# Buffers from the general pool for the first weight splits at three stage borders, and no split ordered behind the residual, in a two-layer encoder on one core

## The chip, the core and the metric

The kernel runs on one core of a Trainium2 chip. The metric is the device time of one execution in microseconds (us). The kernel before was run three times: 2235.65, 2235.11 and 2233.4 us, median 2235.11. PE is TensorE (the matmul engine), DVE VectorE, ACT ScalarE, POOL GpSimd, SP the engine whose queue issues the weight loads.

## The reference

Two layers of an encoder on 256 tokens of width 2048, in float32. Cut to what matters here:

```
for l in range(DEPTH):                       # DEPTH = 2
    h = rmsnorm(x, pre_mix_norm[l])
    proj = h @ w_in[l]                       # 2048 -> 4176, to three groups of heads
    mix = concatenate([o_a, o_b, o_c]) @ w_out[l]
    x = x + rmsnorm(mix, post_mix_norm[l])
    h = rmsnorm(x, pre_ffn_norm[l])
    f = (silu(h @ w_gate[l]) * (h @ w_up[l])) @ w_down[l]
    x = x + rmsnorm(f, post_ffn_norm[l])
```

All of x must be summed (rmsnorm over 2048 columns) before any row of the next stage's result is final. The kernel applies the row's scale behind the matmul, so that only the residual itself, not its sum of squares, stands ahead of the next stage's first matmul.

## The kernel before

**Precision.** Each float32 operand of a large matmul is split into a high and a low part in a format that PE takes at full rate: ACT casts it (`hi`), DVE subtracts (`lo = src - hi`). This is `hilo`, lines 327 to 329. A product then takes three matmuls: high x high, low x high, high x low.

**A dense product** (`dense`, from line 337) goes through its weights in units of 1024 columns (two chunks of 128 rows by 512 columns). `unit(u)` loads a unit into a `ws` buffer by SP, splits it into `wh` and `wl`, and `mm` (lines 347 to 355) issues the three matmuls of one chunk and one half of the tokens (t = 0 or 1, 128 tokens each). There are five buffers each of `ws`, `wh` and `wl` (`WSB`, `WHB`), and a general pool of 64 buffers of 512 columns (`U()`), from which activations and their splits come.

**At a stage's border** the old stage's last product is called with `tail=4`: its last four units keep their splits, all matmuls of half 0 come first, `residual(0)` runs on DVE while PE does half 1. The new stage's first product is called with `head=3`: its units 0 to 2 do half 0 alone, half 1 follows behind unit 2, so that PE has work while `residual(1)` runs. There are three such inner borders: mixing to channel mixer of layer 0 (near 399 us), layer 0 to layer 1 (near 1117 us), and mixing to channel mixer of layer 1 (near 1506 us). A unit of the new stage has six matmuls per half.

**The new x** becomes matmul input by quads: `norm_quad` (from line 435) transposes four blocks of 128 columns on PE (L439), multiplies by the gain, and splits. For the very first quad of half 0 it does this block by block (ACT L332, DVE L333), for all others by one DVE product (L448) and `hilo` (L328, L329). x has four quads in each half, eight in all.

**Order.** Each engine takes its instructions in the order that the build has written down. The build places them by its own view of what is ready and by the program's order; a tile's buffer is given in the order in which the program asks for one of that kind. Where the program says so, an instruction stands behind another one of its engine:

```
for u0, ins in hold:
    if u >= u0:
        order.enter_context(tc.issue_after(ins.ins))
hilo(wh[:, 0:m * n], wl[:, 0:m * n], ws[:, 0:m * n])
```

`hold` is set by `residual(0)` to its last operation, with u0 = 1: at an inner border the low halves of units 1 and 2 stand behind it on DVE. At the program's start `hold` has other entries (lines 112 and 523), which concern the very first product.

**The old stage's end on DVE.** In `out_proj` the evacuation adds the accumulator to the earlier part (L1201, where there are two passes), ACT squares it (L1204), DVE multiplies by the gain (L1205). `residual` then runs a chain of small operations for the row's scale (`rsqrt_sum`, L257 to L270) and four operations on 512 columns (L495).

Of the kernel before, what the change touches and what calls it, by code (L numbers as in the profile page):

```python
# [10 lines left out]
F32R = mybir.dt.float32r  # L11
I32 = mybir.dt.int32
AF = mybir.ActivationFunctionType
ALU = mybir.AluOpType
AX = mybir.AxisListType

P = 128
# [25 lines left out]
WHB = 5  # L43
# [10 lines left out]
def kernel(  # L54
# [8 lines left out]
    act, dve, pe, pool, sync = nc.scalar, nc.vector, nc.tensor, nc.gpsimd, nc.sync  # L63
# [3 lines left out]
    wpool = ctx.enter_context(tc.tile_pool(name="wpool", bufs=3))  # L67
# [5 lines left out]
    def U(dt=F32):  # L73
        return upool.tile([P, 512], dt, tag="u", name="u")
# [37 lines left out]
    hold = [(0, dve.tensor_copy(out=col0, in_=ps[:, 0:16]))]  # L112
# [139 lines left out]
    def rsqrt_sum(v, part, mul, eps, tag):  # L252

        pre = SM(1, tag + "p")
        dve.tensor_reduce(out=pre, in_=v, axis=AX.X, op=ALU.add)  # L257
        dve.tensor_scalar(out=pre, in0=pre, scalar1=eps / mul, scalar2=None, op0=ALU.add)
        w = SM(3, tag + "w")
        z = SM(1, tag + "z")  # L260
        a = SM(1, tag + "a")
        dve.tensor_scalar(out=w[:, 0:1], in0=part, scalar1=pre[:, 0:1], scalar2=64.0 * mul,
                          op0=ALU.add, op1=ALU.mult)
        dve.tensor_scalar(out=z.bitcast(I32), in0=w[:, 0:1].bitcast(I32), scalar1=-0.5,
                          scalar2=float(0x5F3759DF - 2 ** 31), op0=ALU.mult, op1=ALU.add)
        for i in range(1, 3):
            dve.tensor_scalar(out=w[:, i:i + 1], in0=w[:, 0:1], scalar1=4.0 ** -i, scalar2=None, op0=ALU.mult)
        for i in range(3):
            dve.scalar_tensor_tensor(out=a, in0=z, scalar=w[:, i:i + 1], in1=z, op0=ALU.mult, op1=ALU.mult)
            dve.scalar_tensor_tensor(out=z, in0=a, scalar=-3.0, in1=z, op0=ALU.add, op1=ALU.mult)  # L270
        return z
# [55 lines left out]
    def hilo(hi, lo, src):  # L327
        act.copy(out=hi, in_=src)  # L328
        dve.tensor_tensor(out=lo, in0=src, in1=hi.bitcast(F32), op=ALU.subtract)  # L329
# [7 lines left out]
    def dense(lhs, ks, n, load, evac, ch=2, need=None, pre=None, head=0, mid=None, tail=0,  # L337
              after0=None):

        acc = [psa.tile([P, 512], F32, tag="acc", name="acc") for _ in range(NT)]
        nu = -(-len(ks) // ch)
        held = []

        def mm(t, c, u, kc, wh, wl):
            i = u * ch + c
            rh = wh[:, c * n:(c + 1) * n]
            rl = wl[:, c * n:(c + 1) * n]  # L350
            xh, xl = lhs(kc[c], t)
            o = acc[t][:, 0:n]
            pe.matmul(o, xh, rh, start=(i == 0), stop=False)  # L353
            pe.matmul(o, xl, rh, start=False, stop=False)  # L354
            pe.matmul(o, xh, rl, start=False, stop=(i == len(ks) - 1))  # L355

        def unit(u):
            kc = ks[u * ch:(u + 1) * ch]
            m = len(kc)
            ws = wpool.tile([P, 1024], F32, tag="ws", name="ws", bufs=WSB)  # L360
            wv = ws[:, 0:m * n].rearrange("p (c n) -> p c n", c=m)
            load(wv, kc[0], m)
            wh = wpool.tile([P, 1024], F32R, tag="wh", name="wh", bufs=WHB)
            wl = wpool.tile([P, 1024], F32R, tag="wl", name="wl", bufs=WHB)
            with ExitStack() as order:
                if u < head:
                    for u0, ins in hold:
                        if u >= u0:
                            order.enter_context(tc.issue_after(ins.ins))
                hilo(wh[:, 0:m * n], wl[:, 0:m * n], ws[:, 0:m * n])  # L370
            if need is not None:
                for k in kc:
                    bg.ensure(*need(k))
            return u, kc, wh, wl

        for u in range(nu):
            a = unit(u)
            if head <= u < nu - tail:
                for c in range(len(a[1])):
                    for t in range(NT):  # L380
                        mm(t, c, *a)
            else:
                for c in range(len(a[1])):
                    mm(0, c, *a)
                held.append(a)
                if u == head - 1 and mid is not None:
                    mid()
                if u == nu - 1:
                    if pre is not None:
                        pre()  # L390
                        pre = None
                    evac(0, acc[0][:, 0:n])
                if u in (head - 1, nu - 1):
                    for h in held:
                        for c in range(len(h[1])):
                            mm(1, c, *h)
                    held.clear()
            bg.step(BUDGET)
        if pre is not None:
            pre()  # L400
        if after0 is not None:
            after0()
        for t in range(1 if tail else 0, NT):
            evac(t, acc[t][:, 0:n])
# [85 lines left out]
    def residual(t, parts, ssqp, rname):  # L490

        r = rsqrt_sum(ssqp[t][:, 0:3], ssqp[t][:, 3:4], 1.0 / DM, EPS, rname)
        for c in range(4):
            xv = xs[:, t, c * 512:(c + 1) * 512]
            ins = dve.scalar_tensor_tensor(out=xv, in0=parts[(c, t)], scalar=r[:, 0:1], in1=xv,  # L495
                                           op0=ALU.mult, op1=ALU.add)
        if t == 0:
            hold[:] = [(1, ins)]

    def post_weight(ap, l):  # L500
        w = [U() for _ in range(4)]
# [6 lines left out]
    for l in range(DEPTH):  # L508
# [677 lines left out]
        def out_proj(lhs, passes, w, wpm, rname, need, after0):  # L1186
            parts = {}
            ssqp = [SM(4, "ssqp0"), SM(4, "ssqp1")]
            for i, ks in enumerate(passes):
                last = i == len(passes) - 1  # L1190
                for nb in range(4):
                    if i == 0:
                        parts[(nb, 0)], parts[(nb, 1)] = U(), U()

                    def ev(t, ps):
                        o = parts[(nb, t)]
                        if not last:
                            act.copy(out=o, in_=ps)
                            return
                        if i > 0:  # L1200
                            dve.tensor_tensor(out=o, in0=o, in1=ps, op=ALU.add)  # L1201
                            ps = o
                        junk = U()
                        act.activation(out=junk, in_=ps, func=AF.Square, accum_out=ssqp[t][:, nb:nb + 1])  # L1204
                        dve.tensor_tensor(out=o, in0=ps, in1=wpm[nb], op=ALU.mult)  # L1205
                        if nb == 3:
                            residual(t, parts, ssqp, rname)
                    dense(lhs, ks, 512, wload(w, nb * 512, 512), ev, need=need,
                          **(dict(tail=TAILG, after0=after0) if last and nb == 3 else {}))
# [251 lines left out]
```

## Time and profile before

| | |
|---|---|
| runs | 2233.4 to 2235.65 us, median 2235.11 |
| profiled execution | 2234.73 us, its span 2233.0 us |
| mean granted clock of TensorE | 0.998 |
| busy: PE, PEld, DVE, ACT | 99%, 82%, 79%, 53% |
| chain that ended last: PE, DVE, DMA | 92%, 5%, 1% |

The page gives the busy time of each engine and the chain of work that ended last. Views of the trace give more: what an engine waited for, the instructions of an engine in order of time (start, duration, line, operation, output and inputs), and busy times in a stretch. "Busy" on PE is modelled from starts: back to back, matmuls of 512 columns start every 0.227 us, though each is shown with 0.39 us.

### The profile page before, as it was taken

The numbers are of one execution on the slowest core, as the hardware profiler recorded it, in microseconds if no ns is written. First come the engines' busy times: TensorE is split into PE (matmuls) and PEld (weight loads), VectorE is DVE, ScalarE is ACT, GpSimd is POOL, SyncE is SP. The second block draws the span as 40 slices with busy tenths as digits, with TensorE's granted clock in tenths as the row PEclk, the third lists the DMA queues.
The fourth block names the chain that finished last, engine by engine and source line by source line (L and its number), as shares of the span: only waits on it lengthen the run. The fifth ranks groups of instructions, "written<-read, shape, count | busy, mean of one in ns | idle before, by whom it ended". The sixth has DMA issues, their size and how long they took to land.

```text
span 2233.0 us, 29215 instructions
## 1 busy us (share of the span) xinstructions
PE 2203.0 (99%) x10483; PEld 1839.3 (82%) x10483; DVE 1762.0 (79%) x2873; ACT 1182.5 (53%) x1642; POOL 45.9 (2%) x93
## 2 busy tenths in 40 slices
PE   8999999999999999999999999999999999999998
PEld 7988887788888888888879888877888888888886
DVE  6777998899999897544486779979999998975444
ACT  6665545555555555444356655455555555554432
POOL 2000000000000000000000000000000000000000
PEclk9999999999999999999999999999999999999999
DMA  7554525546656656555556545245565566665553
GB/s 254 171 178 146 188 89 162 162 164 207 217 181 217 225 189 223 171 195 192 179 172 186 183 142 171 97 153 161 188 207 208 191 215 214 202 214 178 191 196 124
DMA packets 218545, 407.75 MB, mean 183 GB/s; under 512 B 17607, under 2 KB 30065, under 8 KB 218400
## 3 DMA queue, kind: packets, MB, share of 16 engines
q1 hardware_dynamic: 215360, 397.72, 54.3%
q0 software_dynamic: 3008, 8.16, 1.3%
q8 instruction: 82, 1.34, 0.2%
q14 instruction: 63, 0.52, 0.1%
q10 hardware_dynamic: 32, 0.01, 0.0%
HBM read 402.94 MB, written 2.90 MB: 182 GB/s over the span
## 4 chain that ended last, share of the span: by engine, by line
PE 92%; DVE 5%; DMA 1%; issue 0%; ACT 0%; SPq 0%; DVEq 0%; ACTq 0%; POOLq 0%
PE acc L1306 19%; PE tp L1306 19%; PE acc L353 16%; PE acc L354 16%; PE acc L355 16%; DVE wl L329 1%; DVE xs L495 1%; PE tp L1230 1%; PE tp L1051 1%; DVE u L950 1%; DMA cd<-u 1%; PE tp L795 0%; PE tp L802 0%; PE tp L1022 0%; DMA xs<-in_x_dram 0%
## 5 line engine op out<-in xcount | busy, mean ns | idle before, releaser
L328 ACT CAST wh<-ws 128x1024 fp32r<-128x1024 f32 (+3 forms) x820 | 815.5, 1010 | 795.2 <-PE acc L354 409.6
L329 DVE TENSOR_TENSOR wl<-ws,wh 128x1024 fp32r<-128x1024 f32 (+3 forms) x820 | 942.1, 1170 | 336.2 <-ACT wh L328 332.2
L353 PE MATMUL acc<-wh,u 128*128 128x512 f32 (+2 forms) x1792 | 695.5, 389 | 0.4
L354 PE MATMUL acc<-wh,u 128*128 128x512 f32 (+2 forms) x1792 | 686.2, 383 | 3.5 <-DVE u L329 1.8
L355 PE MATMUL acc<-wl,u 128*128 128x512 f32 (+2 forms) x1792 | 685.6, 383 | 3.0 <-DVE wl L329 3.0
L354 PEld LDWEIGHTS acc<-wh,u 128*128 128x128 f32 x1792 | 337.5, 188 | 68.4 <-DVE u L333 4.1
L355 PEld LDWEIGHTS acc<-wl,u 128*128 128x128 f32 x1792 | 336.8, 188 | 68.1 <-DVE wl L329 5.8
L353 PEld LDWEIGHTS acc<-wh,u 128*128 128x128 f32 x1792 | 337.3, 188 | 62.3 <-ACT u L332 2.5
L1306 PE MATMUL acc<-wh,u 128*128 128x512 f32 x1220 | 376.4, 389 | 0.0
L1306 PE MATMUL tp<-wh,u 128*128 128x512 f32 x1220 | 375.8, 389 | 0.0
L1306 PEld LDWEIGHTS acc<-wh,u 128*128 128x128 f32 x1220 | 228.7, 188 | 47.9 <-DVE u L329 0.6
L1306 PEld LDWEIGHTS tp<-wh,u 128*128 128x128 f32 x1220 | 228.9, 188 | 47.6
L1306 PE MATMUL acc<-wl,u 128*128 128x512 f32 x610 | 237.4, 389 | 0.0
L1306 PE MATMUL tp<-wl,u 128*128 128x512 f32 x610 | 237.3, 389 | 0.0
L1306 PEld LDWEIGHTS acc<-wl,u 128*128 128x128 f32 x610 | 114.5, 188 | 23.7
L1306 PEld LDWEIGHTS tp<-wl,u 128*128 128x128 f32 x610 | 114.5, 188 | 23.7
L950 DVE SCALAR_TENSOR_TENSOR u<-u,cols 128x241 f32<-128x241 f32 (+14 forms) x240 | 101.0, 470 | 0.0
L1344 ACT CAST wh<-ws 128x1024 fp32r<-128x1024 f32 x60 | 63.0, 1050 | 28.4 <-PE tp L1306 12.8
L1345 DVE TENSOR_TENSOR wl<-ws,wh 128x512 fp32r<-128x512 f32 x60 | 41.1, 686 | 23.8 <-ACT wh L1344 21.8
L328 ACT CAST u<-u 128x512 fp32r<-128x512 f32 (+2 forms) x48 | 27.8, 587 | 38.2 <-DVE u L448 34.2
L1329 ACT ACTIVATE u<-u,sm 128x512 f32<-128x512 f32 x40 | 28.8, 724 | 34.6 <-DVE u L1376 24.4
L1351 DVE TENSOR_TENSOR ws<-ws 128x512 f32<-128x512 f32 x60 | 41.5, 692 | 2.0
(303 smaller groups left out, 1541.8 us busy)
## 6 DMA issues: line engine op xcount, KB each, us to landing
ws<-in_w_gate_dram SPq DMA_DIRECT2D x176, 512.0 KB, 5.0
ws<-in_w_up_dram SPq DMA_DIRECT2D x176, 512.0 KB, 4.8
ws<-in_w_down_dram SPq DMA_DIRECT2D x176, 512.0 KB, 3.6
ws<-in_w_in_dram SPq DMA_DIRECT2D x112, 512.0 KB, 4.3
ws<-in_w_out_dram SPq DMA_DIRECT2D x64, 512.0 KB, 3.7
ws<-in_w_ukv_dram SPq DMA_DIRECT2D x16, 512.0 KB, 3.7
ws<-in_w_uq_dram SPq DMA_DIRECT2D x16, 384.0 KB, 3.5
ws<-in_w_in_dram SPq DMA_DIRECT2D x10, 444.0 KB, 4.1
```

The lines of the kernel that those rows point to most:

```text
L328: act.copy(out=hi, in_=src)
L329: dve.tensor_tensor(out=lo, in0=src, in1=hi.bitcast(F32), op=ALU.subtract)
L353: pe.matmul(o, xh, rh, start=(i == 0), stop=False)
L354: pe.matmul(o, xl, rh, start=False, stop=False)
L355: pe.matmul(o, xh, rl, start=False, stop=(i == len(ks) - 1))
L495: ins = dve.scalar_tensor_tensor(out=xv, in0=parts[(c, t)], scalar=r[:, 0:1], in1=xv, op0=ALU.mult, op1=ALU.add)
L950: dve.scalar_tensor_tensor(out=o, in0=i, scalar=wc, in1=o, op0=ALU.mult, op1=ALU.add)
L1306: pe.matmul(o, a, b, start=count[i] == 1, stop=count[i] == total[i])
L1329: act.activation(out=sg[t], in_=x, func=AF.Silu, scale=rfb[0][:, t:t + 1])
L1344: act.copy(out=wh, in_=wg)
L1345: dve.tensor_tensor(out=wl[:, 0:512], in0=b11, in1=wh[:, 0:512].bitcast(F32), op=ALU.subtract)
L1351: dve.tensor_tensor(out=b21, in0=b21, in1=b22, op=ALU.subtract)
```

## The change

At an inner border (`hold` is empty there now, since `residual` clears it) units 0 to 2 take their split weights from the general pool, one buffer of 512 columns for each chunk's high and low part, and each chunk is split by itself. No split is ordered behind the residual there. All other units, and the program's start, are as before. Lines behind 360 stand five or six further down in the changed kernel: L439 becomes L445, L448 becomes L454, L495 becomes L501, L1201 to L1205 become L1206 to L1210; the matmuls L353 to L355 become L352 to L354.

```diff
-        def mm(t, c, u, kc, wh, wl):
+        def mm(t, c, u, kc, w):
             i = u * ch + c
-            rh = wh[:, c * n:(c + 1) * n]
-            rl = wl[:, c * n:(c + 1) * n]
+            rh, rl = w[c][0][:, 0:n], w[c][1][:, 0:n]
...
-            wh = wpool.tile([P, 1024], F32R, tag="wh", name="wh", bufs=WHB)
-            wl = wpool.tile([P, 1024], F32R, tag="wl", name="wl", bufs=WHB)
             with ExitStack() as order:
                 if u < head:
                     for u0, ins in hold:
                         if u >= u0:
                             order.enter_context(tc.issue_after(ins.ins))
-                hilo(wh[:, 0:m * n], wl[:, 0:m * n], ws[:, 0:m * n])
+                if u < head and not hold:
+
+                    w = [(U(F32R), U(F32R)) for _ in range(m)]
+                    for c in range(m):
+                        hilo(w[c][0][:, 0:n], w[c][1][:, 0:n], ws[:, c * n:(c + 1) * n])
+                else:
+                    wh = wpool.tile([P, 1024], F32R, tag="wh", name="wh", bufs=WHB)
+                    wl = wpool.tile([P, 1024], F32R, tag="wl", name="wl", bufs=WHB)
+                    hilo(wh[:, 0:m * n], wl[:, 0:m * n], ws[:, 0:m * n])
+                    w = [(wh[:, c * n:(c + 1) * n], wl[:, c * n:(c + 1) * n]) for c in range(m)]
...
-            ins = dve.scalar_tensor_tensor(out=xv, in0=parts[(c, t)], scalar=r[:, 0:1], in1=xv,
-                                           op0=ALU.mult, op1=ALU.add)
-        if t == 0:
-            hold[:] = [(1, ins)]
+            dve.scalar_tensor_tensor(out=xv, in0=parts[(c, t)], scalar=r[:, 0:1], in1=xv,
+                                     op0=ALU.mult, op1=ALU.add)
+        hold.clear()
```

Orders move on PE, DVE and ACT, at the three inner borders and in short stretches behind them; POOL's and SP's read as before. Three places at the first border (mixing to channel mixer of layer 0) follow; the third border's read alike, the second's differ in a few rows.

ACT, from the square of the last block's half 0 on, before. `wh_4165`, `wh_4177`, `wh_4251` and `wh_4269` are units 1 to 4 of the new product; `u_4100` is the high part of x's first quad.

```order
L1204 ACTIVATE u_4048,sm_2889<-u_3466 128x512
L328 CAST wh_4165<-ws_4163 128x1024
L328 CAST wh_4177<-ws_4175 128x1024
L328 CAST wh_4251<-ws_4249 128x1024
L328 CAST wh_4269<-ws_4267 128x1024
L332 ACTIVATE u_4100<-tp_4095,cols_91 128x128
L1204 ACTIVATE u_4111,sm_2890<-u_3467 128x512
L332 ACTIVATE u_4100<-tp_4095,cols_91 128x128
L328 CAST u_4151<-u_4153 128x512
```

The same place in the changed kernel. `wh_4281`, `wh_4321`, `wh_4339` and `wh_4357` are units 4 to 7; `u_4142` and `u_4144` are the two chunks of unit 0, `u_4155` is x's second quad, `u_4169` the first chunk of unit 1.

```order
L1209 ACTIVATE u_4048,sm_2889<-u_3466 128x512
L328 CAST wh_4281<-ws_4279 128x1024
L328 CAST wh_4321<-ws_4319 128x1024
L328 CAST wh_4339<-ws_4337 128x1024
L332 ACTIVATE u_4100<-tp_4095,cols_91 128x128
L328 CAST wh_4357<-ws_4355 128x1024
L332 ACTIVATE u_4100<-tp_4095,cols_91 128x128
L1209 ACTIVATE u_4111,sm_2890<-u_3467 128x512
L328 CAST u_4142<-ws_4140 128x512
L332 ACTIVATE u_4100<-tp_4095,cols_91 128x128
L328 CAST u_4144<-ws_4140 128x512
```

Unit 0, which before had been cast ahead of this place, now stands behind the casts of units 4 to 7 and behind the square of half 1.

DVE, from the middle of the scale's chain for half 0 to the first operations on the new x, before (`xs` is x, `wl` the low part of a unit).

```order
L269 SCALAR_TENSOR_TENSOR sm<-sm 128x1
L270 SCALAR_TENSOR_TENSOR sm<-sm 128x1
L495 SCALAR_TENSOR_TENSOR xs<-u,sm,xs 128x512 x4
L1201 TENSOR_TENSOR u<-u,acc 128x512
L333 SCALAR_TENSOR_TENSOR u<-tp,cols,u 128x128
L448 TENSOR_TENSOR u<-tp,cols 128x512
```

The same place in the changed kernel:

```order
L269 SCALAR_TENSOR_TENSOR sm<-sm 128x1
L329 TENSOR_TENSOR wl<-ws,wh 128x1024
L270 SCALAR_TENSOR_TENSOR sm<-sm 128x1
L329 TENSOR_TENSOR wl<-ws,wh 128x1024
L269 SCALAR_TENSOR_TENSOR sm<-sm 128x1
L270 SCALAR_TENSOR_TENSOR sm<-sm 128x1
L269 SCALAR_TENSOR_TENSOR sm<-sm 128x1
L1206 TENSOR_TENSOR u<-u,acc 128x512
L270 SCALAR_TENSOR_TENSOR sm<-sm 128x1
L501 SCALAR_TENSOR_TENSOR xs<-u,sm,xs 128x512 x4
L333 SCALAR_TENSOR_TENSOR u<-tp,cols,u 128x128
L329 TENSOR_TENSOR wl<-ws,wh 128x1024
```

The splits of units 4 and 5 (`wl`) and the sum of the last accumulator now stand ahead of the residual, the split of unit 6 right behind it.

PE, the end of the old stage and the first rows of the new one, before:

```order
L355 MATMUL acc<-wl,u 128x512
L439 MATMUL tp<-ident,xs 128x128 x10
L353 MATMUL acc<-wh,u 128x512
L439 MATMUL tp<-ident,xs 128x128 x2
L354 MATMUL acc<-wh,u 128x512
```

In the changed kernel twelve transposes come first, then fourteen matmuls of half 0 with weights from the general pool (units 0 and 1, and two of unit 2), of which these are the last two, and what follows:

```order
L352 MATMUL acc<-u 128x512
L353 MATMUL acc<-u 128x512
L445 MATMUL tp<-ident,xs 128x128 x12
L354 MATMUL acc<-u 128x512
L352 MATMUL acc<-u 128x512
L353 MATMUL acc<-u 128x512
L354 MATMUL acc<-u 128x512
L352 MATMUL acc<-wh,u 128x512
```

Before, PE has thirty matmuls of half 0 (units 0 to 4) ahead of half 1's transposes; now it has fourteen, then twelve transposes, then the rest of unit 2, and then units 3 and on (`wh`).

## Rows read from the trace of the kernel before

**Rows 1.** The page: span, and PE's busy time, share and instructions.
```profile
span 2233.0 us, 29215 instructions
...
PE 2203.0 (99%) x10483; PEld 1839.3 (82%) x10483; DVE 1762.0 (79%) x2873; ACT 1182.5 (53%) x1642; POOL 45.9 (2%) x93
```

**Rows 2.** Waits of PE, 398 to 425 us: waiter, releaser: us, times, longest.
```profile
PE acc L355 <- DVE wl L329: 1.5, 3, 0.9
PE acc L354 <- DVE u L333: 0.4, 2, 0.2
PE acc L354 <- DVE u L329: 0.2, 1, 0.2
```

**Rows 3.** Timeline of PE, first border: start, us, engine, line, operation, [idle before].
```profile
399.25 0.39 PE L355 MATMUL acc<-wl,u 128*128 128x512 f32 x1
399.48 1.27 PE L439 MATMUL tp<-ident,xs 128*128 128x128 f32 x10
400.86 0.50 PE L353 MATMUL acc<-wh,u 128*128 128x512 f32 x1
...
415.64 0.50 PE L354 MATMUL acc<-wh,u 128*128 128x512 f32 x1 [0.23 <-DVE u L329]
```

**Rows 4.** Stretch 399.48 to 415.64: length, busy us (instructions) of PE, PEld, DVE...
```profile
399.48:415.64 16.16, 13.70 (x64) 8.70 (x62) 15.47 (x34) 4.78 (x10) 0.00 (x0) 1.00 0.43 130
```

**Rows 5.** Timeline of DVE, first border.
```profile
396.76 0.22 DVE L269 SCALAR_TENSOR_TENSOR sm<-sm 128x1 f32<-128x1 f32 x1
...
398.11 2.75 DVE L495 SCALAR_TENSOR_TENSOR xs<-u,sm,xs 128x512 f32<-128x512 f32 x4
400.76 0.69 DVE L1201 TENSOR_TENSOR u<-u,acc 128x512 f32<-128x512 f32 x1
401.36 0.35 DVE L333 SCALAR_TENSOR_TENSOR u<-tp,cols,u 128x128 fp32r<-128x128 f32 x1
...
404.41 1.22 DVE L329 TENSOR_TENSOR wl<-ws,wh 128x1024 fp32r<-128x1024 f32 x1
```

**Rows 6.** Timeline of ACT, first border.
```profile
395.59 2.24 ACT L328 CAST wh<-ws 128x1024 fp32r<-128x1024 f32 x2
...
401.49 0.63 ACT L1204 ACTIVATE u<-u 128x512 f32<-128x512 f32 x1 [0.68 <-DVE u L1201]
...
402.12 0.35 ACT L332 ACTIVATE u<-tp,cols 128x128 fp32r<-128x128 f32 x1
402.36 0.61 ACT L328 CAST u<-u 128x512 fp32r<-128x512 f32 x1
```

**Rows 7.** Weight buffers `ws`, 380 to 425 us: from a load's issue to its landing.
```profile
DMA to landing us min/median/max: 3.6/4.4/4.7
```

**Rows 8.** Timelines of PE, DVE and ACT, second border.
```profile
1117.02 1.25 PE L439 MATMUL tp<-ident,xs 128*128 128x128 f32 x10
1118.36 0.50 PE L353 MATMUL acc<-wh,u 128*128 128x512 f32 x1
...
1131.91 0.50 PE L354 MATMUL acc<-wh,u 128*128 128x512 f32 x1 [0.22 <-DVE u L329]
...
1114.89 2.74 DVE L495 SCALAR_TENSOR_TENSOR xs<-u,sm,xs 128x512 f32<-128x512 f32 x4
...
1114.27 1.06 ACT L328 CAST wh<-ws 128x1024 fp32r<-128x1024 f32 x1 [0.30 <-PE acc L354]
```

**Rows 9.** Loads of 1100 to 1145 us: KB each, median us to landing.
```profile
ws<-in_w_in_dram SPq DMA_DIRECT2D x14, 512.0 KB, 3.9
```

**Rows 10.** Stretch 304 to 308 us; the last three: granted clock, DMA share, GB/s.
```profile
304.00:308.00 4.00, 3.61 (x15) 2.82 (x16) 3.37 (x9) 2.43 (x4) 0.00 (x0) 0.75 0.09 26
```

**Rows 11.** Timeline of PE in two stretches of the mixing stage.
```profile
284.32 1.99 PE L1051 MATMUL tp<-u 128*128 128x256 f32 x8
...
304.13 0.72 PE L1044 MATMUL tp<-ident,u 128*128 128x128 f32 x4 [1.28 <-DVE u L1039]
...
305.67 3.32 PE L1051 MATMUL tp<-u 128*128 128x256 f32 x8
```

More of the change, by code (lines that the diff above doesn't have):

```diff
@@ L373, in unit @@
                     bg.ensure(*need(k))
-            return u, kc, wh, wl
+            return u, kc, w
         for u in range(nu):
```

## The prediction

> **What bounds the kernel now.** Read the page first: PE is busy for 2203.0 of 2233.0 us [rows 1], so the kernel is as long as its matmuls, and a change can win or lose only where PE stands still or is fed late. The diff touches three such places, where one stage hands over to the next: near 399 us (mixing to channel mixer of layer 0), 1117 us (layer 0 to layer 1) and 1506 us (mixing to channel mixer of layer 1). I call them borders and number a stage's weight units from 0, so that units 0 to 2 are the ones the change treats.
>
> The list of what PE waited for at the first border is short: 1.5 us for low halves of split weights, 0.4 and 0.2 us for halves of the normalised x [rows 2]. The timeline gives the rest. The old stage's last matmul starts at 399.25, transposes of the new x follow at once at 399.48, the first matmul of the new stage is at 400.86, and from 415.64 on PE runs without a gap [rows 3]. In that stretch PE took up 64 instructions [rows 4]; without the old stage's last one these are 32 transposes (8 of x's eight quads of four blocks) and 31 matmuls: five units of six for token half 0, and the first of half 1. That count is what I compare against.
>
> Why is nothing lost before 399.48? On DVE the chain of small operations for residual half 0 reaches its middle at 396.76 and the four residual operations start at 398.11, 0.66 us apiece; the first is there at 398.11 + 0.69 = 398.80 [rows 5], before PE has finished the old stage. DVE takes up the sum of the last old accumulator (a 0.69 us operation) only behind the residual, at 400.76 [rows 5]. ACT casts two weight units in a row from 395.59 to 397.83 [rows 6], into buffers that the old stage gives up. From 400.76 on DVE is the busy engine and PE's waits are waits for it.
>
> **The change, part by part.** Nine casts and nine subtractions of 1024 columns become eighteen of 512 each. A subtraction of 1024 columns lasts 1.22 us, an operation of 512 lasts 0.69; the next one starts 0.09 before its end (400.76 to 401.36), so that they take 1.13 and 0.60 of the queue [rows 5]. Each pair costs 0.07 us more, nine of them 0.6 us of DVE in all, inside the walk below. No DMA is added.
>
> The removed wait matters less than the place where the operations now stand. In the order of the changed kernel the new splits of units 0 to 2 are not early. Units 3 to 7 now get the five wh/wl buffers, and their splits come first. Two of them (units 4 and 5) stand on DVE inside the residual's chain, and so does the sum of the old accumulator. On ACT the casts of units 4 to 7 stand ahead of the first cast for unit 0. And since units 0 to 2 keep three of the five ws buffers, units 6 and 7 can be loaded only when DVE has split units 4 and 5. So ACT, first in first out, waits for loads. I walk the first border with these rows.
>
> *DVE up to the residual.* To 396.98 as before. Split of unit 4 to 398.1; unit 5's cast ends at 397.83 [rows 6], so its split runs to about 399.35. Three dependent small operations of 0.2 to 0.25 us; then the 0.60 us sum, whose matmul has ended by 399.64 [rows 3]. Together 2 x 1.13 + 0.60 = 2.86 us are put ahead of the residual; it starts at 398.11 + 2.86 = 401.0, and its first result is there at 401.7. PE's transposes start at 401.7 instead of 399.48: **2.2 us late**; some of the inserted work fills gaps between dependent small operations, so 1.9 is the low end.
>
> *ACT up to the first matmul.* Unit 6's load is issued at 398.1 and lands 4.4 us later (3.6 to 4.7 here [rows 7]), at 402.5; cast 1.06 [rows 8] to 403.55; one normalising operation (0.24); unit 7's load, issued at 399.4, landed at 403.8, cast to 404.85; normalising 0.24, the square with its read-out 0.63, unit 0's cast 0.61 [rows 6]: 406.35. PE's first matmul comes at 406.4 instead of 400.86: **5.5 us late**. What waits behind those casts is everything on ACT for the new x, and so DVE's partner operations.
>
> *From there until PE is full.* DVE, after the residual (403.65): normalising 0.26 (behind ACT, 404.1), split of unit 6 to 405.2, normalising to 405.5, old-stage product 0.60 to 406.4 (behind the square), unit 0's two low halves at 407.1 and 408.3, quad 1's product to 409.2, split of unit 7 to 410.5, quad 1's low half to 411.2, unit 1's low halves at 411.9 and 412.6, residual half 1 (2.65) to 415.2, unit 2's first low half at 415.9. PE can do only 6 + 6 + 2 matmuls before that last one, because its queue has them in this order, and 12 + 12 transposes; from 416.0 on it is full, since units 3 to 7 are split long before. Against the count of before at 415.64, 31 - 14 = 17 matmuls at 0.227 us (399.25 to 399.48 [rows 3]) and 32 - 24 = 8 transposes at about 0.11 us (1.27 us for ten, with the last one's tail [rows 3]) are still to do: 17 x 0.227 + 8 x 0.11 + 0.36 = **5.1 us**. With the load at 3.6 us DVE comes out 0.5 us earlier, so the lower bound is 4.6; at 4.7 us some 0.3 more, 5.4.
>
> *The other borders.* The third has the rows of the first, 1106.76 us later, and the same order: 5.1. At the second the order is alike, but the accumulator's sum doesn't stand in the chain. Its residual starts at 1114.89 + 2.26 = 1117.2, the transposes 0.8 us late. Unit 5's cast ends at 1115.33 [rows 8], loads take 3.9 us here [rows 9], so unit 6 lands at 1119.3 and unit 7 at 1120.6; with the square between their casts unit 0's cast ends near 1122.8, against a first matmul at 1118.36 [rows 8]. With the same 9.6 us from there PE is full at 1132.45, against 1131.91: 17 x 0.227 + 8 x 0.11 + 0.54 = 5.3.
>
> **Sum:** 5.1 + 5.3 + 5.1 = 15.5 us. The profiled execution took 2234.73 us (its span is 2233.0 [rows 1]); with 15.5 it is 2250.2. The median of the runs shown, 2235.11, lies 0.4 above it: **2250.6 us**. Between the borders the order is the same but for single rows, where PE is covered by splits two to four units ahead; I cost that at nothing, and if the cover failed, one late split (1.22 us) per border would be the size of it.
>
> **A rule for the change.** Of PE's waits three, 1.5 us at one border, end on a low half [rows 2], at the same place in all three borders. The Trainium skill, page "Perfetto Trace Analysis", section "Optimization Strategy", says that the same bubble repeating on the engine that should be saturated can mean that there is not enough SBUF for the next tile. By that the twelve buffers added at each border would take the waits away.
>
> **The rivals.**
> *Faster: the buffers feed PE.* If units 0 to 2 were split under the old stage's end, the waits of 2.1 us [rows 2] would go at three borders: 6.3 us, 2228.8. For it: buffers and loads are there. Against it: engines take their queues in order, and unit 0's cast stands behind loads that can't start before 398. It decides if ACT's cast of unit 0 ends by about 401. Chance 4%.
> *No change.* PE's late start is made up, because units 3 to 7 lie ready and PE later needs none of DVE's splits; before, DVE is busy beside it. That needs 5 us of idle PE after the border, and there are no gaps after 415.64 [rows 3]. 2235, chance 4%.
> *Only the residual is late.* If the loads of units 6 and 7 don't hold ACT and DVE catches up, 2.2 + 0.8 + 2.2 = 5 to 6 us remain: 2241. Chance 8%.
> *The clock falls too.* Where PE had waited 1.28 us and done little else, from 304 to 308 us, the mean granted clock was 0.75, so for part of it at 1.2 GHz [rows 10], and eight small matmuls of L1051 took 3.32 us instead of 1.99 [rows 11]; with the next matmuls some 1.6 us. The new gap (about 403.5 to 406.4, with no PE work) is emptier. Three times 1.6 is 4.8: 2255.4. The page "TensorE: Matmul & The Clock Gate" of the Trainium skill, Part 1, has the rule that the clock is let down after idling; the row agrees. Against the price: while PE waits for DVE until 416, slower matmuls are hidden. Chance 12%.
>
> **How the numbers follow.** The forecast has the remaining 72%, between 2247.5 and 2252.5: bounds of 4.6 and 5.4 a border, and 0.4 on either side for waits between engines that I rounded, so 3 x 4.2 to 3 x 5.8 over 2235.1. The range is 2244 to 2256.5: it takes in the forecast, the clock's case and a part of the cheaper one. What a measurement can tell from no change is 0.2%, 4.5 us. So slower 0.92, same 0.04, faster 0.04.
>
> **What will show it.** At each border, PE waits for the residual (0.7 to 2 us), then about 3 us for ACT's cast of unit 0, near 1.8 us for that of unit 1, and some 1 and 0.7 us for low halves of units 1 and 2; ACT idles for 3 to 4 us with casts of units 6 and 7 behind loads issued after 398. Wrong would be: first matmul before 402, or waits as long as these but PE full before 413.

## The result and the profile after

Six runs of the changed kernel have a median of 2251.95 us (2250.45 to 2254.39), six of the kernel before beside them 2234.68 us (2233.37 to 2238.51). The ratio is 1.0078, 95% interval [1.0068, 1.0089]: 17.3 us slower. The profiled execution took 2251.55 us, its span is 2249.8 us, 16.8 above the span of before [rows 1]. The page's first part:

```profile
span 2249.8 us, 29223 instructions
...
PE 2206.6 (98%) x10483; PEld 1843.4 (82%) x10483; DVE 1764.7 (78%) x2882; ACT 1183.0 (53%) x1651; POOL 45.9 (2%) x93
```

DVE's busy time rose by 2.7 us and ACT's by 0.5, for nine more instructions each, so the added work is far too little for the loss. What PE waited for, over the whole span (total, times, longest):

```profile
PE acc L352 <- ACT u L328: 13.8, 7, 3.3
PE tp L445 <- DVE xs L501: 4.4, 3, 1.9
...
PE acc L354 <- DVE u L329: 2.1, 5, 0.8
```

Matmuls with `u` on both sides are those with weights from the general pool: PE now waits 13.8 us for their casts. Before, no wait for a cast or for the residual stood among the waits of the first border [rows 2]. PE's timeline at the first border (start, duration, line, idle before):

```profile
398.88 0.39 PE L354 MATMUL acc<-wl,u 128*128 128x512 f32 x1
401.13 1.95 PE L445 MATMUL tp<-ident,xs 128*128 128x128 f32 x12 [1.86 <-DVE xs L501]
406.38 0.50 PE L352 MATMUL acc<-u 128*128 128x512 f32 x1 [3.30 <-ACT u L328]
...
410.60 0.79 PE L352 MATMUL acc<-u 128*128 128x512 f32 x1 [1.30 <-ACT u L328]
...
412.10 0.80 PE L354 MATMUL acc<-u 128*128 128x512 f32 x1 [0.28 <-DVE u L329]
412.69 0.63 PE L352 MATMUL acc<-u 128*128 128x512 f32 x1
413.12 0.63 PE L353 MATMUL acc<-u 128*128 128x512 f32 x1
...
414.81 1.47 PE L445 MATMUL tp<-ident,xs 128*128 128x128 f32 x12
416.04 0.48 PE L354 MATMUL acc<-u 128*128 128x512 f32 x1
```

Counted from the old stage's last matmul, the transposes start 2.25 us behind it (before 0.23 [rows 3]) and the first matmul 7.50 us behind it (before 1.61). From 416.04 on PE is full. ACT says why the first cast is late:

```profile
395.22 2.24 ACT L328 CAST wh<-ws 128x1024 fp32r<-128x1024 f32 x2
401.60 1.05 ACT L328 CAST wh<-ws 128x1024 fp32r<-128x1024 f32 x1 [4.14 <-DMA ws<-in_w_gate_dram]
402.55 0.36 ACT L332 ACTIVATE u<-tp,cols 128x128 fp32r<-128x128 f32 x1
403.90 1.04 ACT L328 CAST wh<-ws 128x1024 fp32r<-128x1024 f32 x1 [0.99 <-DMA ws<-in_w_gate_dram]
...
405.72 0.60 ACT L328 CAST u<-ws 128x512 fp32r<-128x512 f32 x1
```

The casts of units 4 to 7 (`wh`) come first, those of units 6 and 7 after 4.14 and 0.99 us of waiting for their loads; unit 0's (`u`) is last, at 405.72. DVE meanwhile:

```profile
396.53 1.22 DVE L329 TENSOR_TENSOR wl<-ws,wh 128x1024 fp32r<-128x1024 f32 x1
...
397.73 1.22 DVE L329 TENSOR_TENSOR wl<-ws,wh 128x1024 fp32r<-128x1024 f32 x1
...
400.24 2.74 DVE L501 SCALAR_TENSOR_TENSOR xs<-u,sm,xs 128x512 f32<-128x512 f32 x4
```

Two splits stand ahead of the residual, which starts at 400.24 (before 398.11 [rows 5]).

Where the 16.8 us of span lie is read from four stretches: span's start to the old stage's last matmul at the first border, from there to the same matmul at the second, from the second to the third, and from the third to the span's end. Before, these matmuls start at 399.25, 1116.80 and 1506.01; in the changed kernel at 398.88, 1121.82 and 1516.52. The stretches differ by -0.4, +5.4, +5.5 and +6.3 us: one loss of 5 to 6 us behind each border. The first stretch holds no border, and it varies by up to 2.2 us between the runs, so spans alone tell little.

A shorter ruler leaves out what happens far from a border: from the old stage's last matmul to the 96th matmul behind it, the last one of the new stage's first product (eight units, twelve matmuls each). At the first border the 96th is, before and after,

```profile
430.30 0.39 PE L355 MATMUL acc<-wl,u 128*128 128x512 f32 x1
```

```profile
435.46 0.39 PE L354 MATMUL acc<-wl,u 128*128 128x512 f32 x1
```

so 31.05 us before (from 399.25) and 36.58 after (from 398.88). The differences at the three borders are 5.5, 5.3 and 6.3 us, 17.2 in all: the whole loss lies within 38 us behind each border. "Lost at the borders" below is by this ruler; a table for all runs stands behind the experiments.

### The profile page after: what moved, and what is told of

Read it like the earlier page. It is cut to its first block, busy times and chain, and to the rows that moved or that the text cites. A ratio compares the mean times of both kernels' runs of the same rounds, so it can differ in the third digit from the quotient of the medians.

```text
span 2249.8 us, 29223 instructions
## 1 busy us (share of the span) xinstructions
PE 2206.6 (98%) x10483; PEld 1843.4 (82%) x10483; DVE 1764.7 (78%) x2882; ACT 1183.0 (53%) x1651; POOL 45.9 (2%) x93
## 4 chain that ended last, share of the span: by engine, by line
PE 93%; DVE 4%; DMA 2%; issue 1%; ACT 1%; SPq 0%; DVEq 0%; ACTq 0%; POOLq 0%
PE tp L1311 18%; PE acc L1311 18%; PE acc L352 16%; PE acc L354 16%; PE acc L353 16%; DVE wl L329 1%; DMA ws<-in_w_in_dram 1%; PE tp L1235 1%; PE tp L1056 1%; DVE u L955 1%; DMA cd<-u 1%; PE tp L800 0%; PE tp L807 0%; PE tp L1027 0%; DMA ws<-in_w_gate_dram 0%
## 5 line engine op out<-in xcount | busy, mean ns | idle before, releaser
L328 ACT CAST wh<-ws 128x1024 fp32r<-128x1024 f32 (+3 forms) x811 | 806.2, 1009 | 815.7 <-PE acc L353 408.6
L352 PE MATMUL acc<-wh,u 128*128 128x512 f32 (+2 forms) x1756 | 681.7, 389 | 0.5 <-ACT u L328 0.5
L353 PE MATMUL acc<-wh,u 128*128 128x512 f32 (+2 forms) x1756 | 670.6, 382 | 0.3 <-DVE u L333 0.3
L354 PE MATMUL acc<-wl,u 128*128 128x512 f32 (+2 forms) x1756 | 670.5, 382 | 0.0
L354 PEld LDWEIGHTS acc<-wl,u 128*128 128x128 f32 x1756 | 330.0, 188 | 61.5
L353 PEld LDWEIGHTS acc<-wh,u 128*128 128x128 f32 x1756 | 330.8, 188 | 59.4 <-DVE u L329 0.8
L352 PEld LDWEIGHTS acc<-wh,u 128*128 128x128 f32 x1756 | 330.5, 188 | 59.2 <-ACT u L328 1.3
L1311 PEld LDWEIGHTS acc<-wh,u 128*128 128x128 f32 x1220 | 228.8, 188 | 47.4
L1311 PEld LDWEIGHTS acc<-wl,u 128*128 128x128 f32 x610 | 114.5, 188 | 23.9
L329 DVE TENSOR_TENSOR u<-u 128x512 fp32r<-128x512 f32 (+2 forms) x48 | 30.9, 652 | 15.9 <-ACT u L328 15.9
```

The costliest lines, as they stand in the source:

```text
L1311: pe.matmul(o, a, b, start=count[i] == 1, stop=count[i] == total[i])
```

## The experiments

My theory: the head units (0 to 2) get the general pool's buffers late in the build's order, so that the splits of units 3 to 7 overtake theirs on ACT and DVE. Rivals: the removed ordering behind the residual (A), the splits cut into 512 columns (B), the loads through five `ws` buffers (C), the fall of the clock (D).

One thing is read from the orders alone: with the buffers as in the change and the ordering behind the residual kept, the build writes the same order on all five engines as for the changed kernel. With these buffers the removed ordering moves nothing.

**The other half alone.** The kernel before without the ordering:

```diff
...
-        if t == 0:
-            hold[:] = [(1, ins)]
...
+        hold.clear()
```

> The change's second half alone: the weight splits of the head units no longer wait for the residual at the inner borders, and the buffers wh and wl stay as they were. My theory (the general pool's buffers come late, so that the splits of units 3 to 7 stand ahead of those of units 0 to 2 on ScalarE and VectorE): the lost wait plays hardly a part, the kernel stays within 2 us of the kernel before (some 2235 to 2237 us), and the first matmul of the first border starts within 1 us of 400.9. Rival A (the splits that no longer wait for the residual push the residual back, and this is what costs): at least half of the change's 17 us is here, 2243 us or more, and PE waits for the residual's xs some 2 us at each border.

Measured: 2235.84 us, ratio 1.0011 [1.0002, 1.002], some 2.3 us by medians (the kernel before beside it: 2233.53). The time is in the range I gave, a little over the 2 us, and the picture isn't what I expected. PE's timeline at the first border:

```profile
403.00 1.29 PE L439 MATMUL tp<-ident,xs 128*128 128x128 f32 x8 [3.88 <-DVE xs L495]
404.08 0.67 PE L353 MATMUL acc<-wh,u 128*128 128x512 f32 x1
```

PE waits 3.88 us for the residual, twice as long as in the changed kernel, and the first matmul comes at 404.08, not near 400.9. Rival A's wait is there, its price is not: behind this border only 1.2 us are lost, and 0.1 us behind the second, where PE waits 1.7 us. DVE has done four splits ahead of the residual that it needn't do later, and from 404 on PE has nothing to wait for but 0.4 us for x and 0.2 us for the residual of half 1. A wait in a list isn't a loss, where the same work only changes places.

**Later units behind the head's.**

```diff
...
+                elif last and u < head + 5:
+                    for ins in last:
+                        order.enter_context(tc.issue_after(ins.ins))
...
```

(`last` holds the cast and the subtraction of unit 2's last chunk.)

> The changed kernel, with the splits of units 3 to 7 of the first product behind a border ordered on ScalarE and VectorE behind the split of unit 2. My theory (overtaking by the later units is a large part of the loss, the pool's late buffers are the rest): 6 to 10 us faster than the changed kernel, some 2242 to 2246 us, with ScalarE's idle time for the gate weights' loads (4.1 and 1.0 us at the first border) gone from ahead of unit 0's cast. Rival B (the instructions cut to 512 columns and their number are what costs): no gain, 2251 us or more. Rival C (the five buffers of loads cost): no gain or a loss, since a load's buffer is then given back no earlier.

Measured: 2245.31 us, ratio 1.0051 [1.0039, 1.0064]: 11.8 us over the kernel before beside it, against 17.3 for the change, so a third of the loss is gone (5.5 us by medians, somewhat under the 6 to 10 expected). The five runs lie far apart, 2242.66 to 2249.63 us, and the profiled one (2242.89) is among the fastest. The transposes start right behind the old stage (397.54, last matmul 397.31), and the loads no longer hold ACT. But unit 0's cast still stands behind the first quad's work on ACT, and the later units, which nothing has split by then, are now late too:

```profile
398.18 0.37 ACT L333 ACTIVATE u<-tp,cols 128x128 fp32r<-128x128 f32 x1 [4.43 <-PE tp L449]
...
400.68 0.60 ACT L328 CAST u<-ws 128x512 fp32r<-128x512 f32 x1
...
406.72 1.99 ACT L328 CAST wh<-ws 128x1024 fp32r<-128x1024 f32 x2
```

ACT idles 4.43 us ahead of the first quad, with unit 0's cast behind it in its queue. Overtaking is a part; how large a part, this run doesn't measure, since it makes the later units late as well.

**Where the buffers come from: a pair.** The first has eight buffers of its own for units 0 and 1, the second takes the same eight from the general pool; in both, unit 2 uses `wh` and `wl` and the pool has 56 buffers. The first against the changed kernel:

```diff
-UB = 64
+UB = 56
...
-                if u < head and not hold:
+                if u < min(head, 2) and not hold:
-                    w = [(U(F32R), U(F32R)) for _ in range(m)]
+                    w = [[wpool.tile([P, 512], F32R, tag="hs", name="hs", bufs=8) for _ in range(2)] for _ in range(m)]
```

> The changed kernel with the same four 512-column splits for units 0 and 1 and with no wait for the residual, but into eight buffers of their own in place of the general pool's (unit 2 goes back to wh and wl, and the general pool is 8 buffers smaller to make room). My theory (where the buffers come from decides): within 3 us of the kernel before, 2234 to 2238 us, no wait of PE at the borders over 1.5 us. Rival B (512-column instructions and their number): 2243 us or more, as the count for these units is that of the change. Rival A (no wait for the residual): 2243 us or more too.

> The pair to the run with own buffers, different from it only in that units 0 and 1 take their eight buffers from the general pool (as small as there, 56). My theory: 12 to 16 us slower than that run, some 2247 to 2252 us, with PE waiting 2 us or more for ScalarE's cast at each border. Rivals A and B: the two runs of the pair agree within 2 us.

Measured: 2238.02 us, ratio 1.0016 [1.0007, 1.0025], and 2251.81 us, ratio 1.0081 [1.0068, 1.0093]. The pair differs by 13.8 us, and the buffers' source is its only difference (with own buffers there are eight more in all). ACT's casts of unit 0 and 1 in the first (`hs`), and the first cast of unit 0 and of its second chunk in the second (`u`):

```profile
381.08 1.14 ACT L328 CAST hs<-ws 128x512 fp32r<-128x512 f32 x2 [0.77 <-DMA ws<-in_w_gate_dram]
...
383.67 1.14 ACT L328 CAST hs<-ws 128x512 fp32r<-128x512 f32 x2 [0.49 <-DMA ws<-in_w_gate_dram]
```

```profile
404.01 0.61 ACT L328 CAST u<-ws 128x512 fp32r<-128x512 f32 x1
...
406.26 0.61 ACT L328 CAST u<-ws 128x512 fp32r<-128x512 f32 x1
```

With their own buffers the head is split over 20 us earlier, beside the old stage's matmuls. Rival B falls: both runs have the same 512-column instructions for units 0 and 1, and the first loses 2.7 us at the borders, the second 15.8. Three expectations missed. The first run is 4.5 us above the kernel before beside it, not within 3. In it PE waits 3.9 us for the residual, over the 1.5 I allowed; the losses there are 0.5 us at the first border and 2.3 at the third, where TensorE's granted clock also fell for longer (mean 0.66 from 1510 to 1520 us, against 0.57 from 402 to 406). In the second run PE's wait for the casts, expected at 2 us or more at each border, is 1.6, 2.7 and 1.6 us; at the first and third it waits 2.9 us for the residual as well.

**More load buffers** (`WSB = 8`, and 58 for 64 in the pool).

> The changed kernel with eight load buffers (ws) in place of five, paid for by six buffers of the general pool (58 for 64). ScalarE should then no longer idle for the gate weights' loads ahead of unit 0's cast at the first border (4.1 and 1.0 us in the changed kernel). My theory: what costs is that the casts of later units stand ahead, and that unit 0's own buffers come late, not the loads: only 1 to 4 us faster than the changed kernel. Rival C (the loads cost, as the 5.1 us of idle time read): 3 x 4 to 5 us faster than the changed kernel, within 4 us of the kernel before.

Measured: 2248.94 us, ratio 1.0064 [1.0052, 1.0077], 15.7 us over the kernel before beside it against 17.3 for the change. ACT's waits for the gate weights at the border are gone:

```profile
397.29 1.04 ACT L328 CAST wh<-ws 128x1024 fp32r<-128x1024 f32 x1 [0.31 <-PE acc L353]
402.44 0.37 ACT L332 ACTIVATE u<-tp,cols 128x128 fp32r<-128x128 f32 x1 [4.11 <-PE tp L445]
...
403.71 0.61 ACT L328 CAST u<-ws 128x512 fp32r<-128x512 f32 x1
```

Instead ACT waits 4.11 us for the first transpose, since DVE now has four splits ahead of the residual, and unit 0's cast comes at 403.71. Counted from the old stage's last matmul (397.04 here) that is 6.67 us, in the changed kernel 6.84. At the borders 4.6, 5.8 and 4.8 us are lost, 15.2 in all against 17.2. Rival C, which wanted 12 to 15 us back, falls: with the loads' wait gone, another wait of nearly the same length stands in its place. What the loads would cost if nothing took their place, the run doesn't show.

**The clock.** Behind PE's gap the granted clock fell to its lower level. Stretches of the three borders in the changed kernel (length, PE busy and count, granted clock, DMA share, GB/s):

```profile
404.00:406.00 2.00, 0.00 (x0) 1.00 0.29 25
...
408.00:410.00 2.00, 1.25 (x3) 0.50 0.34 24
410.00:412.00 2.00, 1.22 (x2) 0.50 0.79 247
412.00:416.00 4.00, 3.90 (x17) 0.65 0.80 223
...
1126.00:1130.00 4.00, 1.88 (x5) 0.77 0.47 132
1130.00:1134.00 4.00, 2.14 (x7) 0.80 0.61 151
...
1528.00:1532.00 4.00, 3.66 (x8) 0.50 0.84 242
```

0.50 is 1.2 GHz: PE had nothing at all from 404 to 406 us, and by 408 the clock is down. At the lower level matmuls of 512 columns start 0.43 us apart (412.69 to 413.12 above), for 0.227. The Trainium skill, page "TensorE: Matmul & The Clock Gate", Part 1, has the rule that idling lets the clock down; the trace agrees. What it costs here, the next run measures, with matmuls that do nothing of use in the gap (`turned` holds the transposes so far):

```diff
...
+            if u == 0 and head and not hold:
+                lhs(0, 0)
+                with tc.issue_after(turned[-1].ins):
+                    for _ in range(4):
+                        pe.matmul(acc[1][:, 0:512], ident, xs[:, 0, 0:512], start=True, stop=True)
...
```

> The changed kernel with four idle matmuls (identity by the new residual, into an accumulator that is started afresh behind them) in PE's gap between the first transposes and the first matmul of each inner border, where PE waited 3.3 us at the first. The granted clock is then to stay at its upper level through the border's first matmuls. My theory: PE has to wait for the casts and low halves anyway, so the time stays within 2 us of the changed kernel whether the clock stays up or not. Rival D (the fall of the clock behind the gap is a large part of the loss): 4 us or more faster than the changed kernel.

Measured: 2248.57 us, ratio 1.0065 [1.0052, 1.0079]. That is 15.4 us over the kernel before beside it, against 17.3 for the change: 1.9 us gained, within the 2 us of my theory, short of the 4 of rival D, and the intervals of the two ratios overlap. The fillers take the gap, and the clock stays at 2.4 GHz at the second and third border; at the first it falls only behind the next waits, from about 410 us:

```profile
400.82 3.60 PE L388 MATMUL acc<-xs,ident 128*128 128x512 f32 x8
```

```profile
410.00:412.00 2.00, 1.42 (x3) 0.52 0.82 215
...
1126.00:1130.00 4.00, 2.48 (x11) 1.00 0.57 148
...
1528.00:1532.00 4.00, 3.36 (x20) 1.00 0.74 236
```

At the borders it gains 0.0, 0.0 and 1.0 us on the changed kernel, of 17.2. The first border says nothing of the price, since the clock falls there in both runs. At the second and third PE is full from these matmuls on, in the changed kernel and then with fillers:

```profile
1137.55 0.50 PE L354 MATMUL acc<-u 128*128 128x512 f32 x1 [0.55 <-DVE u L329]
...
1534.53 0.47 PE L354 MATMUL acc<-u 128*128 128x512 f32 x1
```

```profile
1136.01 0.50 PE L354 MATMUL acc<-u 128*128 128x512 f32 x1 [0.55 <-DVE u L329]
...
1531.59 0.50 PE L354 MATMUL acc<-u 128*128 128x512 f32 x1 [0.54 <-DVE u L329]
```

Counted from the old stage's last matmul (1121.82 and 1516.52; with fillers 1120.30 and 1514.58) these are 15.73 against 15.71 us at the second border: PE waits 0.55 us for DVE in both, so that the slow matmuls cost nothing. At the third they are 18.01 against 17.01: there the clock stayed down so long that PE itself was late, and its wait for DVE is gone. The run also moves four transposes, so 1.0 is a rough figure.

**Own buffers, and the ordering kept.** Units 0 and 1 in two pairs of 1024 columns of their own (`hh`, `hl`), the pool at 56, all else as before; and, beside it, the kernel before with the pool at 56 alone.

> The idea of the change in the form that should cost nothing: units 0 and 1 get 1024-column buffers of their own, two pairs, the wait for the residual stays, the general pool shrinks by 8. My theory: within 1 us of the kernel before on either side, since the first matmul of the border waits for the residual and its transposes there, not for wh and wl: -1 to +1 us. The change's hope (the shared wh and wl buffers hold the border up): 2 us or more faster than before.

> Control: the kernel before with 56 buffers in its general pool for 64, nothing else. Every theory: the same time as the kernel before, within 0.5 us; if it is slower, the runs with a smaller pool are to be read against this one.

Measured: 2235.95 us, ratio 1.0008 [0.9999, 1.0017], and 2235.62 us, ratio 1.0008 [0.9999, 1.0017]. Neither is clear of the kernel before, and they don't differ from one another. By medians they are 2.7 and 2.4 us slower, more than the 1 and 0.5 expected, but the intervals reach no change, and at the borders neither loses anything in all. If the smaller pool costs some 2 us elsewhere, which isn't shown, they are a part of the 4.5 us of the run with own buffers too. Against the rule weighed ahead of the prediction, from the Trainium skill's "Perfetto Trace Analysis", section "Optimization Strategy": here the repeating bubble did not come from too few buffers; given own ones, the kernel gains nothing, and given the general pool's it loses 17 us. With own buffers and the ordering PE still waits 1.9 us for a low half (`hl`) at the first border, and without the ordering, in the first run of the pair, for none:

```profile
404.51 0.50 PE L355 MATMUL acc<-hl,u 128*128 128x512 f32 x1 [1.94 <-DVE hl L330]
```

**The pool's buffers, asked for earlier.** Is it the pool, or the place? This run takes units 0 and 1 from the general pool (64 buffers, as in the change), but loads and splits them ahead of the old product's last four units (rival E: the pool has no buffers to spare there):

```diff
...
         for u in range(nu):
+            if tail and u == nu - tail and soon:
+                nload = soon.pop()
+                for v in range(EARLYU):
+                    ws = wpool.tile([P, 1024], F32, tag="ws", name="ws", bufs=WSB)
+                    nload(ws.rearrange("p (c n) -> p c n", c=2), 2 * v, 2)
+                    w = [(U(F32R), U(F32R)) for _ in range(2)]
+                    for c in range(2):
+                        hilo(w[c][0], w[c][1], ws[:, c * 512:(c + 1) * 512])
+                    split.append(w)
             a = unit(u)
...
```

> Units 0 and 1 take their eight buffers from the general pool as in the run with two units from the pool, but the program asks for them, loads and splits them earlier: ahead of the last four units of the old stage's last product. My theory now (the build gives the general pool's buffers, and with them the place on each engine, in the program's order, and it is this late place that costs, not the pool): 2234 to 2240 us, within 4 us of the run with own buffers, no wait of PE over 1.5 us for a split at the first border. Rival E (the pool has no buffers to spare at the border, and someone is made to wait for them): 2245 us or more.

Measured: 2235.9 us, ratio 1.0013 [1.0004, 1.0021]. All but some 2 us of the loss is gone, with the pool as the source. ACT's four casts of both units, and PE at the border:

```profile
388.80 2.17 ACT L330 CAST u<-ws 128x512 fp32r<-128x512 f32 x4
```

```profile
401.91 1.94 PE L458 MATMUL tp<-ident,xs 128*128 128x128 f32 x8 [4.28 <-DVE xs L514]
```

The pool had the buffers to spare; the place in the program decides. Rival E falls. What is left is the residual: PE waits 4.28 us for it, since four splits stand ahead of it on DVE, and the borders lose 0.8, -0.1 and 1.0 us.

**And the residual prompt.** The same, with unit 2 in `wh` and `wl` and its low half ordered behind the residual as before.

> The run before this one, and unit 2 keeps wh and wl with its low half ordered behind the residual, as in the kernel before. My theory: 0 to 3 us faster than the kernel before, 2230.5 to 2233.5 us, since the residual is prompt again and units 0 and 1 lie ready, so that of PE's waits of some 2 us at each border a part goes. If the residual's promptness is worth nothing: the same as the run before this one.

Measured: 2230.91 us against 2233.53 for the kernel before beside it, ratio 0.9991 [0.9982, 1.0]: 2.6 us faster than the kernel before, with no change at the interval's edge. At the borders it gains 0.8, 0.2 and 0.8 us. The transposes follow the old stage at once, and a part of before's 2.1 us of waits at this border [rows 2] is gone:

```profile
PE acc L355 <- DVE u L335: 1.2, 3, 0.7
PE acc L355 <- DVE u L331: 0.6, 1, 0.6
```

What all runs lose against the kernel before, us: at the three borders, from the old stage's last matmul to the 96th behind it, their sum, and the whole span.

| run | border 1 | border 2 | border 3 | sum | span |
|---|---|---|---|---|---|
| the change | 5.5 | 5.3 | 6.3 | 17.2 | 16.8 |
| no ordering | 1.2 | 0.1 | 1.6 | 2.9 | 2.8 |
| later units behind the head's | 3.4 | 3.1 | 4.2 | 10.7 | 8.2 |
| own buffers, two units | 0.5 | -0.1 | 2.3 | 2.7 | 3.4 |
| pool, two units | 4.7 | 5.6 | 5.5 | 15.8 | 17.4 |
| eight load buffers | 4.6 | 5.8 | 4.8 | 15.2 | 14.7 |
| fillers on PE | 5.5 | 5.3 | 5.4 | 16.2 | 13.9 |
| own buffers, ordering kept | -0.3 | 0.6 | -0.7 | -0.5 | -0.2 |
| before, pool 56 | 0.0 | -0.1 | 0.0 | -0.1 | -0.7 |
| pool, asked for early | 0.8 | -0.1 | 1.0 | 1.6 | 1.3 |
| the same, ordering kept | -0.8 | -0.2 | -0.8 | -1.7 | -3.4 |

Each is one profiled execution. The control (before, pool 56) shows how far a figure at a border can be trusted: it is off by no more than 0.1 us.

## Why the prediction was right

**The sum.** 15.5 us were forecast, 17.3 measured by medians. By borders the terms were 5.1, 5.3 and 5.1 against 5.5, 5.3 and 6.3: the second is right, the first low by 0.4 us, the third by 1.2. The sum holds no term for the clock, whose fall stood among the rivals, and the third border's shortfall is mostly that.

**Residual.** Forecast 2.2 us late, 1.9 at the low end. It is 2.0 (2.25 against 0.23 behind the old stage). That this lateness is a step of the loss was not right: the runs without the ordering and with the pool asked early have twice the wait and lose 0.8 to 1.6 us at the first and third border and nothing to speak of at the second.

**First matmul.** Forecast 5.5 us late, it is 5.9; ACT's order, the waits for the loads of units 6 and 7 and unit 0's cast behind them stand as the walk had them. But the walk hung the size on the loads, and the run with eight load buffers took those waits away for 2 us of 17: DVE's splits ahead of the residual and the late transposes then held unit 0's cast as long. The loads were one of two chains of nearly the same length. What holds is the order: the head's splits are last in both queues.

**PE full.** Forecast 416.0, it is 416.04. That the two agree so closely is in part luck: counted from the old stage's last matmul it is 17.16 us against 16.75 forecast, 0.4 late, about as much as the first matmul. At the second border it is 15.73 against 15.65. The waits are those forecast: 1.86 for the residual, 3.30 and 1.30 for the casts of units 0 and 1, and 0.21 and 0.28 for low halves, where I had 1 and 0.7; matmuls 0.43 us apart filled some of that time.

**The clock.** Its fall, held unlikely as a cost, happened at every border. The price I gave, 1.6 us each, is too high at the second, where the fall cost nothing, as the text put against it: PE waits for DVE in any case. At the third it is some 1.0 us, most of what that border's term was short of; there PE is full 18.0 us behind the old stage's last matmul, against 17.2 at the first, where the clock came back sooner. At the first its price was not measured.

**The rule's reading.** That PE's waits end on a low half "at the same place in all three borders" is not so at the second. Before, PE waited there for a low half of x, not of the weights:

```profile
PE acc L354 <- DVE u L329: 1.4, 2, 1.2
```

**The removed wait** was said to matter less than the place of the operations. With these buffers it moves no instruction; alone it costs some 2.3 us.

**What stays open.** In the changed kernel the buffers of unit 0's two high parts were last read by a matmul of the mixing stage, L862, which at that stage ran from 330.35 to some 334 us: they lay free for over 60 us. Why the build gives them so late was not found. Asking for the twelve buffers ahead of the old stage's last product, with the splits where they were, left the order the same on all five engines; only splits written earlier moved it. How the loss divides among the places on ACT and DVE and PE's own order, which moved with them, is not shown either.

## What to carry to other kernels

Where a build writes each engine's order from the program's, a new buffer source is a new place in every queue that its writers stand in: compare the orders before counting buffers, and look for work that is needed last and now stands first. Move the splits in the program, not to another pool. An idle time's named releaser (a load, the residual) is the last wait in a chain, so remove it in a run before it is priced.

## What the runs showed of the hardware that was not expected

A fall of TensorE's clock behind a gap of 3.1 to 3.3 us, with matmuls of 512 columns 0.43 us apart for 0.227, cost nothing at the second border (clock 0.77 and 0.80 over 8 us), where PE had to wait 0.55 us for DVE at the end anyway, and about 1 us at the third (0.50 from 1528 to 1532), where it hadn't. Matmuls that do nothing of use, put in the gap, held the clock at 1.00 through these two borders; at the first it fell to 0.52 later, behind waits of 1.60 and 0.77 us.
